# Layer 0's keys: turned once, copied to both partition halves by transfers, with the instruction order fitted anew

## Chip, core and metric

The kernel runs on one core of one Trainium2 chip. The metric is the time of one execution in device microseconds, start-up and end included. TensorE is called PE below, VectorE DVE, ScalarE ACT, GpSimd POOL and SyncE, which here only issues transfers, SP.

## What is computed

Two transformer layers over 512 tokens and a width of 1024, in float32. Layer 0 projects the normed input at once to sparse attention (A), with an indexer that picks 128 keys for each query, and to a sliding window attention (B). The keys are few: one head of A (`ak`), one of the indexer (`ik`), two of B (`bk`), 64 wide each, normed per head and rotated.

```python
ak = _rope(_rms_norm(ak.reshape(bsz, seq, 1, HEAD_DIM), a_k_gain), pos)[:, :, 0]
ik = _rope(_rms_norm(ik.reshape(bsz, seq, 1, IDX_DIM), idx_k_gain), pos)[:, :, 0]
bk = _rope(_rms_norm(bk.reshape(bsz, seq, B_KV_HEADS, HEAD_DIM), b_k_gain), pos)
...
rel = jax.nn.relu(jnp.einsum('bqhd,bsd->bqhs', qib, k_idx, preferred_element_type=jnp.float32))
score = jnp.einsum('bqhs,bqh->bqs', rel, wib.astype(jnp.float32)) * idx_scale
_, sel = lax.top_k(score, top_k)
```

Layer 1 has a dilated attention (C) and a differential attention (D) in the same places. After each layer a gated embedding is added to x.

## The kernel before

Every projection is split into a high and a low part of each operand and done as three products (`PASSES`), so that a weight slab of 128 rows (`raw`, 256 KB) is loaded by SP, split by ACT (high) and DVE (low) into `w`, and used by 12 matmuls of 512 columns: four output banks (`mm`, a ring of four) by three products.

`small_evac` takes the projection of the keys, one token tile of 128 after another in the order 1, 2, 3, 0. For each tile ACT copies 256 columns out of the bank, DVE and POOL norm them, DVE rotates them (`rope`) and writes the four heads **twice side by side** into a tile `z` of 512 columns, PE turns the four blocks of 128 columns (`tk`), and `put_heads` splits the bank of 512 columns, by ACT and by DVE, straight into `kTe`, the pair of tiles (high and low; `slot_145` and `slot_146` in the rows) that holds each key head in both halves of the partitions. The two halves are needed because the queries lie stacked, high in one half and low in the other. `scores` multiplies a query tile (`slot_113`, `slot_114` for the indexer) by the high and by the low keys into the banks `sk`, two of them in a ring.

The order of the instructions is not that of the text. `Program.add` records every call; `order` plays them through its own table of costs and lets each engine take the ready call of lowest rank. The rank is the place in the text minus a lead, which `LEADS` gives for each part of the program, 340 numbers in all. What each engine then executes is fixed, and so is SP's queue: a transfer that waits holds all behind it.

Between the projections of layer 0 stand the index scores (`index`), the selection on DVE (`select`, top 8 at a time) and the attentions (`attend_b`, `attend_a`). In layer 1 the queries of C (`put_far`) go to memory outside the core (`far`) and are fetched back, head pair by head pair, into tiles `q` (`fetch`).

The lines that the steps of the prediction touch:

```python
def put_heads(dst, t, bank):
    hi, lo = [d[:, :, t * P:(t + 1) * P] for d in dst]
    hilo(hi, lo, bank.rearrange("p (k n) -> p k n", k=4))
...
for c in range(2):
    nc.tensor.matmul(bank[:, :n], qT[j][:, p, qb * P:(qb + 1) * P],
                     kT[c][:, kv, key0 * P:key0 * P + n], start=c == 0, stop=c == 1)
```

Of the kernel before, what the change touches and what calls it, by code (L numbers as in the profile page):

```python
# [12 lines left out]
F32 = mybir.dt.float32  # L13
F32R = mybir.dt.float32r
BF16 = mybir.dt.bfloat16
AF = mybir.ActivationFunctionType
ALU = mybir.AluOpType
# [4 lines left out]
P = 128  # L22
# [4 lines left out]
HD = 64  # L27
# [1 line left out]
BIG = 1.0e30  # L29
GONE = -3.0e38  # L30
LEADS = {
    "att": (4, -1, -195, 26, -126, -326, 0, 214, 0, -171, 2, -255, 491, 23, 86, 12, -149, -103, -372, -13, 0, 4, 0, 0,
# [6 lines left out]
    "idx": (33, 43, -69),  # L39
    "mm": (1, 0, 41, -21, 0, -176, 0, 52, -54, 153, 2, 35, 58, 30, 82, 132, 16, -89, 217, 26, 163, -16, 219, -103, 0,  # L40
         2, 0, 32, 0, 10),
    "norm": (-7, -21, -1139, -422, 0, 163, 0, -1317, 0, -65, -255, 143, -554, 273, -6, 8, -797, 9, 343, 0, 45, 356,
         -448, -537),
    "rows": (18, -35, -52, -88),
    "rs": (-21, 0, -68),
    "ss": (0, 163, 0, -7, -4, 5, -8, -12, -47, -11, -20, 23, -71, 120, -103, 27, 0, 119, 63, 0, 144, 4, -6, 7, -774,
         -11, 355, 173, 169, -114, 0, -21),
    "tab": (444, 0, -16, -8, -33, -399),
    "top": (0, -62, -529, -1020, 86, -1, -9, -2, 184, -26, -53, -1657),
    "w": (-65, 84, 19, 457, -62, -25, -203, -28, 45, -204, -236, -132, -266, -243, -190, -125, 17, 0, -9, 0, 23, 3, 0,  # L50
         0, 44, 0, -8, -1, 0, 0),
    "x": (0, 254),
    "y": (424, -60, -418, 188, -612, 0, 22, 1, 283, 500, 1278, -7, 3, -30, -328, -184),
    None: -21,
}
VECS = ("a_q_gain", "a_k_gain", "idx_k_gain", "b_q_gain", "b_k_gain", "c_q_gain", "c_k_gain", "d_q_gain", "d_k_gain",
        "d_lambda_q1", "d_lambda_k1", "d_lambda_q2", "d_lambda_k2")
# [4 lines left out]
QB = 2  # L62
# [200 lines left out]
def tile_trunk(ctx: ExitStack, tc: tile.TileContext, a: dict, out: bass.AP):  # L263
    nc = Program(tc)

    const = ctx.enter_context(tc.tile_pool(name="const", bufs=1))
    sb = ctx.enter_context(tc.tile_pool(name="sb", bufs=2))
# [5 lines left out]
    def uid(s):  # L273
        cnt[0] += 1
        return f"{s}{cnt[0]}"
# [4 lines left out]
    def t_bank():  # L280
        return ps.tile([P, 512], F32, name=uid("tk"), tag="tk", bufs=1)
# [10 lines left out]
    def tmp(shape=(P, 512), tag="t", bufs=4, dt=F32):  # L292
        return sb.tile(list(shape), dt, name=uid(tag), tag=tag, bufs=bufs)
# [22 lines left out]
    ident = const.tile([P, P], F32, name="ident")  # L316
# [19 lines left out]
    def hilo(hi, lo, src, gain=None):  # L336
        if gain is None:
            nc.scalar.copy(out=hi, in_=src)
            nc.vector.tensor_tensor(out=lo, in0=src, in1=hi.bitcast(F32), op=ALU.subtract)
        else:  # L340
            nc.scalar.activation(out=hi, in_=src, func=AF.Copy, scale=gain)
            nc.vector.scalar_tensor_tensor(out=lo, in0=src, scalar=gain, in1=hi.bitcast(F32),
                                           op0=ALU.mult, op1=ALU.subtract)
# [206 lines left out]
    def rope(raw, nh, tabc, tabs, normed):  # L550
        if normed:
            sq = tmp()
            nc.scalar.activation(out=sq[:, :nh * HD], in_=raw, func=AF.Square)
            ss = tiny(nh)
            nc.vector.tensor_reduce(out=ss, in_=sq[:, :nh * HD].rearrange("p (h d) -> p h d", h=nh),
                                    axis=AX.X, op=ALU.add)
            hs = rs_pow(ss, nh, HD * EPS)
        else:
            hs = None
        t1 = tmp()  # L560
        t2 = tmp()
        nc.vector.tensor_tensor(out=t1[:, :nh * HD].rearrange("p (h d) -> p h d", h=nh),
                                in0=raw.rearrange("p (h d) -> p h d", h=nh), in1=tabc, op=ALU.mult)
        nc.vector.tensor_tensor(out=t2[:, :nh * HD].rearrange("p (h s d) -> p h s d", h=nh, s=2),
                                in0=raw.rearrange("p (h s d) -> p h s d", h=nh, s=2)[:, :, ::-1, :],
                                in1=tabs.rearrange("p h (s d) -> p h s d", s=2), op=ALU.mult)
        nc.vector.tensor_tensor(out=t1[:, :nh * HD], in0=t1[:, :nh * HD], in1=t2[:, :nh * HD], op=ALU.add)
        return t1, hs

    def heads():  # L570
        return [slot([P, 4, T], F32R) for _ in range(2)]
# [260 lines left out]
    for i in range(2):  # L832
        wr = slot([P, 4, 512])
        nc.sync.dma_start(out=wr[:, :, :456],
                          in_=a["w_small"][i * 512:(i + 1) * 512, :].rearrange("(k p) n -> p k n", p=P))
# [19 lines left out]
    kTe = heads()  # L855
# [5 lines left out]
    def small_evac(t, bank):  # L861
        raw = tmp(tag="raww", bufs=2)
        nc.scalar.activation(out=raw[:, :256], in_=bank[:, :256], func=AF.Copy, scale=rs0[:, t:t + 1])
        nc.scalar.activation(out=Ve[:, (1 + 3 * t) * HD:(4 + 3 * t) * HD], in_=bank[:, 256:448], func=AF.Copy,
                             scale=rs0[:, t:t + 1])
        nc.scalar.activation(out=iw[:, t, :], in_=bank[:, 448:456], func=AF.Copy, scale=rs0[:, t:t + 1])
        y, hs = rope(raw[:, :256], 4, ktab[:, 0, t], ktab[:, 1, t], True)
        z = tmp()
        nc.vector.tensor_tensor(out=z.rearrange("p (h u d) -> p h u d", h=4, u=2),
                                in0=y[:, :256].rearrange("p (h d) -> p h d", h=4).unsqueeze(2).to_broadcast([P, 4, 2, HD]),  # L870
                                in1=hs.unsqueeze(2).unsqueeze(3).to_broadcast([P, 4, 2, HD]), op=ALU.mult)
        b = t_bank()
        for i in range(4):
            nc.tensor.transpose(b[:, i * P:(i + 1) * P], z[:, i * P:(i + 1) * P], ident)
        put_heads(kTe, t, b)

    proj_tok(wsmall, small_evac, order="tok", tiles=(1, 2, 3, 0))

    few = sb.tile([P, 5 * P], F32, name="few", tag="acc12", bufs=1)
# [55 lines left out]
    idx = {qb: index(qb) for qb in (1, 2, 3)}  # L935
# [230 lines left out]
```

## Time and profile before

| | |
|---|---|
| median of 3 runs | 665.43 us (664.82 to 665.44) |
| the profiled execution | 664.71 us, of which its span is 662.8 us |
| PE busy | 654.7 us, 3373 matmuls |
| DVE, ACT, POOL busy | 530.0, 415.1, 63.4 us |
| granted clock of PE | 1.00 all through |

The span runs from the first to the last instruction. Matmuls overlap, so that a PE busy all the time may still stand between two of them; where it stood is read from the starts.

### The profile page before, as it was taken

What the parts mean: (1) busy time and instruction counts of PE and PEld (TensorE: products, weight loads), DVE (VectorE), ACT (ScalarE), POOL (GpSimd) and SP (SyncE); (2) the same over time, 40 slices, a digit from 0 to 9 for tenths busy, and PEclk for the clock granted to TensorE, in tenths of its full rate; (3) what the DMA queues carried; (4) which work ended last, traced back from release to release, by engine and by line L of the source; (5) the groups of instructions that cost most, each with busy time, mean ns of one, the idle gap of its engine ahead of it and who ended that gap; (6) DMA issues with size and microseconds to landing.
All of it is one profiled execution on the core that took longest, in us unless ns stands there. A gap on an engine that the chain in (4) does not pass through costs nothing.

```text
span 662.8 us, 10361 instructions
## 1 busy us (share of the span) xinstructions
PE 654.7 (99%) x3373; PEld 543.9 (82%) x3373; DVE 530.0 (80%) x1246; ACT 415.1 (63%) x937; POOL 63.4 (10%) x46
## 2 busy tenths in 40 slices
PE   9999999999999999999999999999999999999997
PEld 5888787988988888888888877888888888888886
DVE  6799999999997657677678395999997699558555
ACT  6757577989997824565455252885756577466421
POOL 0130232010000000000031040003040000000000
PEclk9999999999999999999999999999999999999999
DMA  9945256352533422342526537454757533341411
GB/s 332 336 101 145 81 136 182 119 137 65 176 95 97 143 84 77 112 146 93 160 78 182 151 113 223 118 153 113 235 158 206 164 115 94 112 117 58 128 64 64
DMA packets 76711, 90.49 MB, mean 137 GB/s; under 512 B 6641, under 2 KB 43889, under 8 KB 76401
## 3 DMA queue, kind: packets, MB, share of 16 engines
q1 hardware_dynamic: 76512, 89.81, 45.0%
q8 instruction: 27, 0.44, 0.3%
q14 instruction: 28, 0.22, 0.1%
q10 hardware_dynamic: 144, 0.02, 0.0%
HBM read 69.36 MB, written 10.49 MB: 120 GB/s over the span
## 4 chain that ended last, share of the span: by engine, by line
PE 88%; DVE 5%; DMA 3%; issue 1%; ACT 1%; POOL 0%; SPq 0%; DVEq 0%
PE mm L259 68%; PE ob L259 7%; PE tk L259 7%; PE sk L259 6%; DMA raw<-in_w_in_even_dram 1%; DVE t L259 1%; DMA q<-far 1%; DVE w L259 1%; DVE acc L259 1%; DVE few L259 1%; DMA raw<-in_w_ple_proj_dram 1%; POOL tiny L259 0%; SPq L259 0%; DMA far<-ql 0%; ACT w L259 0%
## 5 line engine op out<-in xcount | busy, mean ns | idle before, releaser
L259 PE MATMUL mm<-AT,w 128*128 128x512 f32 (+1 forms) x1176 | 291.0, 393 | 0.0
L259 PEld LDWEIGHTS mm<-AT,w 128*128 128x128 f32 x1176 | 212.6, 188 | 40.4 <-ACT t L259 0.2
L259 PE MATMUL mm<-w,AT 128*128 128x512 f32 (+1 forms) x936 | 238.7, 398 | 0.5 <-DVE w L259 0.5
L259 PEld LDWEIGHTS mm<-w,AT 128*128 128x128 f32 x936 | 170.4, 188 | 35.4 <-ACT AT L259 0.7
L259 ACT ACTIVATE w<-raw,gains 128x512 fp32r<-128x512 f32 x96 | 67.8, 720 | 59.4 <-PE mm L259 50.3
L259 DVE SCALAR_TENSOR_TENSOR w<-raw,gains,w 128x512 fp32r<-128x512 f32 x96 | 70.6, 747 | 28.9 <-ACT w L259 28.5
L259 POOL TENSOR_TENSOR tiny<-tiny,mhalf 128x8 f32<-128x8 f32 (+1 forms) x32 | 57.0, 1784 | 317.2 <-DVE tiny L259 291.9
L259 ACT ACTIVATE pr<-pr,nm 128x256 f32<-128x256 f32 (+3 forms) x128 | 68.5, 537 | 14.5 <-DVE nm L259 14.2
L259 ACT CAST w<-raw 128x512 fp32r<-128x512 f32 x79 | 48.0, 619 | 31.5 <-PE mm L259 21.9
L259 DVE TENSOR_TENSOR w<-raw,w 128x512 fp32r<-128x512 f32 x80 | 53.9, 686 | 13.9 <-ACT w L259 13.8
L259 PE MATMUL tk<-ident,pr 128*128 128x128 f32 x256 | 43.1, 273 | 0.0
L259 PE MATMUL sk<-slot,slot 128*128 128x256 f32 (+3 forms) x176 | 41.3, 323 | 0.0
L259 ACT ACTIVATE t<-t 128x512 f32<-128x512 f32 (+1 forms) x33 | 20.2, 615 | 31.0 <-DVE t L259 31.0
L259 PEld LDWEIGHTS ob<-pt,Ve 128*128 128x128 f32 x272 | 36.3, 191 | 3.5 <-ACT pt L259 1.3
L259 PE MATMUL ob<-pt,Ve 128*128 128x128 f32 x272 | 38.5, 276 | 0.4 <-ACT pt L259 0.4
L259 DVE CUSTOM_DVE_ANT_0 pr<-sk,cpack 128x128 f32<-128x128 f32 (+3 forms) x72 | 31.6, 463 | 8.7 <-PE sk L259 8.5
L259 DVE TENSOR_TENSOR t<-raww,tab 128x512 f32<-128x512 f32 x48 | 32.2, 684 | 6.4 <-ACT raww L259 6.1
L259 PEld LDWEIGHTS tk<-ident,pr 128*128 128x128 f32 x256 | 31.5, 141 | 6.1 <-ACT pt L259 0.9
L259 DVE TENSOR_TENSOR t<-mm,rows 128x512 f32<-128x512 f32 (+1 forms) x33 | 22.1, 670 | 14.5 <-PE mm L259 9.7
L259 PEld LDWEIGHTS sk<-slot,slot 128*128 128x128 f32 x176 | 28.7, 189 | 4.9 <-ACT t L259 1.0
L259 ACT COPY pt<-tk 128x512 f32<-128x512 f32 (+3 forms) x56 | 27.3, 488 | 8.5 <-PE tk L259 8.2
L259 DVE TENSOR_TENSOR AT<-slot,AT 128x512 fp32r<-128x512 f32 x40 | 26.9, 686 | 5.3 <-PE mm L259 3.1
(112 smaller groups left out, 806.9 us busy)
## 6 DMA issues: line engine op xcount, KB each, us to landing
raw<-in_w_in_odd_dram SPq DMA_DIRECT2D x64, 256.0 KB, 3.0
raw<-in_w_in_even_dram SPq DMA_DIRECT2D x36, 256.0 KB, 3.2
raw<-in_w_ple_gate_dram SPq DMA_DIRECT2D x32, 256.0 KB, 2.6
q<-far SPq DMA_DIRECT2D x64, 128.0 KB, 3.0
slot<-qh SPq DMA_DIRECT2D x38, 128.0 KB, 2.5
slot<-ql SPq DMA_DIRECT2D x38, 128.0 KB, 2.5
raw<-in_w_out_even_dram SPq DMA_DIRECT2D x16, 256.0 KB, 2.7
raw<-in_w_out_odd_dram SPq DMA_DIRECT2D x16, 256.0 KB, 2.6
```

The costliest lines, as they stand in the source:

```text
L259: getattr(getattr(nc, engine), method)(*args, **kw)
```

## The change

The heads are no longer doubled before the turn. `small_evac` writes the 256 columns once, PE turns two blocks, ACT and DVE split 256 columns into two tiles of the rings `qh` and `ql` (two buffers each, which the queries use too), and eight transfers of 64 partitions bring the two parts, head by head, into both halves of `kTe`. All 340 leads are other numbers, so the whole order moves; of them the first rows are shown.

```diff
 LEADS = {
-    "att": (4, -1, -195, 26, -126, -326, 0, 214, 0, -171, 2, -255, 491, 23, 86, 12, -149, -103, -372, -13, 0, 4, 0, 0,
+    "att": (-356, 8, 0, -362, 3, 213, 0, 36, 2, 14, -4, 0, 111, 0, 0, 166, 44, 3, -398, 0, 0, 10, 8, -1, -2, 0, 115,
...
         y, hs = rope(raw[:, :256], 4, ktab[:, 0, t], ktab[:, 1, t], True)
-        z = tmp()
-        nc.vector.tensor_tensor(out=z.rearrange("p (h u d) -> p h u d", h=4, u=2),
-                                in0=y[:, :256].rearrange("p (h d) -> p h d", h=4).unsqueeze(2).to_broadcast([P, 4, 2, HD]),
-                                in1=hs.unsqueeze(2).unsqueeze(3).to_broadcast([P, 4, 2, HD]), op=ALU.mult)
+        y = y[:, :256]
+        nc.vector.tensor_tensor(out=y.rearrange("p (h d) -> p h d", h=4), in0=y.rearrange("p (h d) -> p h d", h=4),
+                                in1=hs.unsqueeze(2).to_broadcast([P, 4, HD]), op=ALU.mult)
         b = t_bank()
-        for i in range(4):
-            nc.tensor.transpose(b[:, i * P:(i + 1) * P], z[:, i * P:(i + 1) * P], ident)
-        put_heads(kTe, t, b)
+        for i in range(2):
+            nc.tensor.transpose(b[:, i * P:(i + 1) * P], y[:, i * P:(i + 1) * P], ident)
+        parts = [sb.tile([P, 4, P], F32R, name=uid(x), tag=x, bufs=QB) for x in ("qh", "ql")]
+        hilo(parts[0][:, :2], parts[1][:, :2], b[:, :256].rearrange("p (k n) -> p k n", k=2))
+        for d, part in zip(kTe, parts):
+            for u in range(2):
+                for j in range(2):
+                    nc.sync.dma_start(out=d[64 * u:64 * u + 64, j::2, t * P:(t + 1) * P].bitcast(F32),
+                                      in_=part[64 * j:64 * j + 64, :2, :].bitcast(F32))
```

PE before, from the turn of the last key tile (`tk_187`) to the first index scores; `mm_279` to `mm_282` are the banks of the query projection of B:

```order
L259 MATMUL tk_187<-ident,t_186 128x128 x4
L259 MATMUL mm_281<-w_200,AT 128x512 x2
L259 MATMUL mm_282<-w_200,AT 128x512 x3
L259 MATMUL mm_279<-w_202,AT 128x512
L259 MATMUL sk_213<-slot_145,slot_113 128x256
L259 MATMUL sk_214<-slot_145,slot_114 128x256
L259 MATMUL mm_279<-w_202,AT 128x512 x2
L259 MATMUL mm_280<-w_202,AT 128x512
L259 MATMUL sk_213<-slot_146,slot_113 128x256
```

PE now, the same place (`tk_189` turns the keys of tile 0, `tk_167` of tile 2, `tk_178` of tile 3):

```order
L260 MATMUL tk_189<-ident,t_187 128x128 x2
L260 MATMUL mm_286<-w_204,AT 128x512 x3
L260 MATMUL mm_283<-w_206,AT 128x512 x3
L260 MATMUL mm_284<-w_206,AT 128x512 x3
L260 MATMUL tk_167<-ident,t_165 128x128 x2
L260 MATMUL mm_285<-w_206,AT 128x512 x3
L260 MATMUL mm_286<-w_206,AT 128x512 x3
L260 MATMUL mm_283<-w_208,AT 128x512 x3
L260 MATMUL mm_284<-w_208,AT 128x512 x2
L260 MATMUL sk_217<-slot_145,slot_113 128x256
L260 MATMUL sk_218<-slot_145,slot_114 128x256
L260 MATMUL mm_284<-w_208,AT 128x512
```

Before, 6 matmuls stand between the turn and the first scores; now 20 and another turn. The low keys (`slot_146`) are first read 4 matmuls and the turn `tk_178` after that.

SP's queue now, where the keys' transfers stand (in the kernel before, the rows of the key tiles are not there, and the slabs `raw` follow one another):

```order
L260 DMA slot_145<-qh_157 64x2x128 x4
L260 DMA slot_146<-ql_158 64x2x128 x4
L260 DMA raw_211<-in_w_in_even_dram 128x512
L260 DMA raw_213<-in_w_in_even_dram 128x512
L260 DMA raw_215<-in_w_in_even_dram 128x512
L260 DMA raw_327<-in_w_in_even_dram 128x512
L260 DMA slot_145<-qh_190 64x2x128 x4
L260 DMA slot_146<-ql_191 64x2x128 x4
L260 DMA slot_145<-qh_168 64x2x128 x4
L260 DMA slot_146<-ql_169 64x2x128 x4
L260 DMA slot_145<-qh_179 64x2x128 x4
L260 DMA slot_146<-ql_180 64x2x128 x4
```

The 32 transfers stand in two blocks, one of 8 and one of 24, with four slabs between them.

SP's queue in layer 1 before, around the last token tile of C's queries (`far_1033` is tile 0, `far_1066` tile 3; `raw` slabs are of a later projection):

```order
L259 DMA far_1066<-ql_1065 128x512
L259 DMA far_1033<-qh_1031 128x512
L259 DMA raw_1291<-in_w_in_odd_dram 128x512
L259 DMA q_1099<-far_1066 64x4x128 x2
L259 DMA far_1033<-ql_1032 128x512
L259 DMA raw_1293<-in_w_in_odd_dram 128x512
L259 DMA q_1089<-far_1033 64x4x128 x2
```

And now (`far_1037` is tile 0, `far_1070` tile 3):

```order
L260 DMA far_1037<-qh_1035 128x512
L260 DMA far_1070<-ql_1069 128x512
L260 DMA raw_1297<-in_w_in_odd_dram 128x512
L260 DMA far_1037<-ql_1036 128x512
L260 DMA q_1103<-far_1070 64x4x128 x2
L260 DMA q_1093<-far_1037 64x4x128 x2
```

The low part of tile 0 stood behind a slab and the fetch of tile 3; now it stands behind a slab alone, and the fetch of tile 3 comes after it.

On PE, 48 matmuls of 512 columns stood between the turn of tile 0 and the scores that need it (`q_1089`); it is 42 and four of 256 now (`q_1093`). For tile 1, whose scores come first, it was 38, and is 49 now.

## Rows read from the trace of the kernel before

**Rows 1.** The profile's page: busy time, share of the span, instructions of each engine.

```profile
PE 654.7 (99%) x3373; PEld 543.9 (82%) x3373; DVE 530.0 (80%) x1246; ACT 415.1 (63%) x937; POOL 63.4 (10%) x46
```

**Rows 2.** Stretches: length, busy PE, PEld, DVE, ACT, POOL (instructions), clock, DMA share, GB/s.

```profile
60.00:80.00 20.00, 20.00 (x89) 16.06 (x88) 20.00 (x50) 13.49 (x25) 1.44 (x1) 1.00 0.19 54
160.00:180.00 20.00, 19.56 (x135) 17.67 (x134) 19.53 (x65) 19.14 (x60) 0.00 (x0) 1.00 0.63 184
234.00:400.00 166.00, 165.73 (x748) 134.59 (x747) 115.86 (x195) 79.91 (x129) 18.02 (x10) 1.00 0.41 122
```

**Rows 3.** Groups by form, PE: count | busy us, mean ns | idle before.

```profile
L259 PE MATMUL tk<-ident,t 128*128 128x128 f32 x140 | 22.9, 273 | 0.0
```

**Rows 4.** Timeline of PE, key projection: start, length, instruction, count.

```profile
37.51 3.35 PE L259 MATMUL mm<-w,AT 128*128 128x456 f32 x15
40.70 0.60 PE L259 MATMUL tk<-ident,t 128*128 128x128 f32 x4
41.05 2.51 PE L259 MATMUL mm<-w,AT 128*128 128x456 f32 x11
43.40 0.60 PE L259 MATMUL tk<-ident,t 128*128 128x128 f32 x4
43.76 1.99 PE L259 MATMUL mm<-w,AT 128*128 128x456 f32 x8
```

**Rows 5.** Timeline of PE at four places where it stood; in brackets idle time.

```profile
104.21 1.53 PE L259 MATMUL mm<-w,w 128*128 128x512 f32 x6
106.12 1.20 PE L259 MATMUL mm<-w,w 128*128 128x512 f32 x4 [0.37 <-ACT raww L259]
...
164.74 0.28 PE L259 MATMUL sk<-slot,slot 128*128 128x256 f32 x1
165.47 0.71 PE L259 MATMUL ob<-pt,Ve 128*128 128x128 f32 x4 [0.44 <-ACT pt L259]
...
397.28 1.64 PE L259 MATMUL mm<-AT,w 128*128 128x512 f32 x6
399.19 0.71 PE L259 MATMUL sk<-slot,q 128*128 128x256 f32 x4 [0.27 <-issue]
...
411.74 2.03 PE L259 MATMUL mm<-w,AT 128*128 128x512 f32 x8
414.07 0.63 PE L259 MATMUL sk<-slot,q 128*128 128x128 f32 x4 [0.30 <-DMA q<-far]
```

**Rows 6.** The chain that ended last, 100 to 106 us: start, length, what.

```profile
100.34 3.98 DMA raw<-in_w_ple_proj_dram
...
105.40 0.67 ACT raww L259
```

**Rows 7.** The same chain, 402 to 414 us.

```profile
402.21 0.44 PE tk L259 x4
...
407.69 2.80 DMA far<-ql
...
411.19 2.74 DMA q<-far
```

**Rows 8.** Groups by form, DVE, 20 to 62 us.

```profile
L259 DVE TENSOR_TENSOR t<-raww,slot 128x256 f32<-128x256 f32 x8 | 3.2, 418 | 0.0
L259 DVE TENSOR_TENSOR slot<-tk,slot 128x512 fp32r<-128x512 f32 x4 | 2.8, 688 | 0.0
```

**Rows 9.** Tiles qh and raw, 20 to 60 us: ns min/median/max, first and last start.

```profile
L259 SPq DMA_DIRECT2D slot<-qh x6: 590/604/702, 29.7 to 39.0; - x6
L259 ACT CAST qh<-tk x3: 587/587/593, 29.1 to 37.8; 128x512 fp32r<-128x512 f32 x3
...
DMA to landing us min/median/max: 2.4/2.4/2.5
...
L259 SPq DMA_DIRECT2D raw<-in_w_in_even_dram x15: 327/328/787, 22.0 to 59.3; - x15
```

**Rows 10.** Timeline of PE up to the first index scores.

```profile
47.31 2.81 PE L259 MATMUL mm<-w,AT 128*128 128x512 f32 x11
49.95 0.60 PE L259 MATMUL tk<-ident,t 128*128 128x128 f32 x4
50.31 1.65 PE L259 MATMUL mm<-w,AT 128*128 128x512 f32 x6
51.80 0.40 PE L259 MATMUL sk<-slot,slot 128*128 128x256 f32 x2
```

More of the change, by code (lines that the diff above doesn't have):

```diff
@@ L31 @@
 LEADS = {
-    "att": (4, -1, -195, 26, -126, -326, 0, 214, 0, -171, 2, -255, 491, 23, 86, 12, -149, -103, -372, -13, 0, 4, 0, 0,
[6 rows of a table removed]
[L39 to L54, printed above, removed]
+    "att": (-356, 8, 0, -362, 3, 213, 0, 36, 2, 14, -4, 0, 111, 0, 0, 166, 44, 3, -398, 0, 0, 10, 8, -1, -2, 0, 115,
[7 rows of a table added]
+    "idx": (0, -19, -140),
+    "mm": (744, -44, -5, -100, 0, -370, 0, -81, 79, -11, 156, 0, 63, 118, 85, 144, -94, 133, 380, 29, 160, -6, 224,
+         -111, 9, -8, -15, -6, -21, -7),
+    "norm": (99, 644, 67, 0, 1120, 0, -27, -2462, 0, 268, 118, 5, -132, 0, 653, 0, -273, 89, 0, -98, 66, 18, -83,
+         -661),
+    "rows": (-291, -6, -205, -110),
+    "rs": (48, -45, 0),
+    "ss": (56, 44, 20, 128, -125, 746, 0, 9, 0, 88, 0, 160, 2, 370, -83, 163, 257, 0, -6, -43, -94, 9, -21, 0, 0, 265,
+         207, 384, 166, 189, 43, 115),
+    "tab": (-75, 52, 267, 0, 0, 0),
+    "top": (1052, 338, -786, -922, 0, 0, 4, 9, 177, -8, -5, -306),
+    "w": (97, 232, 550, 471, 185, -84, -58, 22, -107, -1, -101, -3, -117, 0, 0, 0, 8, -19, 2, -56, -234, -3, -102, 0,
+         -43, 84, -50, -117, -68, -254),
+    "x": (-619, -91),
+    "y": (108, 650, 0, 321, 2, 0, 12, -131, 2, 57, 0, -74, 756, -1, -273, 1434),
+    None: 170,
 }
```

13 rows, old and new, of the table LEADS are left out of this document.

## The prediction

> **What bounds the kernel now.** I read the page first, then the stretches, then the starts of PE's matmuls. PE is busy 99% of the span [rows 1], and in the long stretches of projection nearly all of it [rows 2]. A matmul lasts longer than the step to the next one, so busy time hides short stands; the starts show them. Rows 10 give the step: eleven matmuls and six matmuls of 512 columns, each after four turns, take 2.64 and 1.49 us up to the next start, so five matmuls are 1.15 us, 0.23 us each. At that step PE has little to lose. I looked for larger gaps between starts and found four that a change of order can touch [rows 5]: 6 matmuls from 104.21 to 106.12 take 1.91 us where 1.38 would do, 0.53 lost; one of 256 columns from 164.74 to 165.47 takes 0.73 instead of 0.12, 0.61 lost; 6 matmuls before 399.19 and 8 before 414.07 lose 0.5 each. That is 2.1 us together. So the time is the sum of PE's steps and about 2 us of stands, with a start and an end that the change leaves as they are. DVE is the second engine: it is busy 20.00 of 20 us from 60 to 80 and 19.53 from 160 to 180 [rows 2], where it selects keys, and ACT joins it there (19.14). Work taken from DVE or ACT pays only where PE waits for it.
>
> **The turns.** Eight of the sixteen go. Rows 4 give the price: from 37.51 to 41.05 there are 15 matmuls and 4 turns in 3.54 us, from 41.05 to 43.76 there are 11 and 4 in 2.71, so a matmul of 456 columns is 0.21 us, and four turns are 0.43 us, 0.108 each. Eight are 0.86 us, and as PE goes from one to the next without a pause, all of it is on the path. A turn's own length is 273 ns [rows 3], but it overlaps the next. The Trainium skill, "TensorE: Matmul & The Clock Gate", Part 4 (PE-mode transpose), gives about 275 ns for a transpose in a kernel; the length agrees, and eight would be 2.2 us by it. The step decides, and the sum goes by 0.86.
>
> **DVE and ACT.** For each of four tiles the multiply that wrote 512 columns and the subtraction of 512 write 256 now: 688 ns becomes 418 [rows 8], 0.27 us each, 2.2 us for the eight. ACT's cast of 512 columns is 587 ns [rows 9] and gets shorter as well. I cost this at nothing: PE's matmuls hide it, except where DVE's selection ends late. It gives slack up to 200 us, and no time by itself.
>
> **The transfers.** They put a new chain between the turn and the index scores: ACT's cast, SP's issues, landing. Before, the cast wrote the keys in place, and 1.85 us after the turn at 49.95 the first scores ran [rows 10]. What hides the chain now is the order: 20 matmuls and two pairs of turns, 20 x 0.23 + 0.43 = 5.0 us, up to the high keys, and 1.4 us more (four matmuls, a pair of turns, two score matmuls of 256) up to the low keys. The chain: the cast starts about 0.5 us after the turn (the last one, at 37.8, began 0.3 after the end of its four turns at 37.51 [rows 4, 9], and two turns are 0.2), lasts 0.3 to 0.59, and then eight issues follow one another on SP, and the last lands 2.4 us after its issue [rows 9]. The trace has no transfer of 64 partitions by two runs. The nearest rows are the slab, of 128 runs like the new ones, 0.33 us of issue, and the queries' transfer of 64 partitions by four runs, 0.60 [rows 9]. With a gap of 0.05 that makes a step of 0.38 or 0.65. At 0.38 the fourth issue lands at 0.9 + 1.1 + 2.4 = 4.4 us (5.0 to spare it) and the eighth at 6.0 (of 6.4): no wait. At 0.65 they land at 5.3 and 7.9: PE waits 0.3, then 1.5 in all. Tile 2 comes eight issues later; its low keys would land 13.1 us after the turn where the order has them read at 10.5, so 2.6 in all; tile 3 has 17 us for 18.3 and so is covered by that wait. So the price is 0 to 2.6 us. I take 0, since the number of runs is the slab's. A gain of its own is excluded, as nothing waits for less. Behind the 24 issues on SP stand four slabs and more for the next projection, which has 8 others in hand; SP is held some 9 us at 0.38, and the slabs before them in the queue wait for DVE's splits, which come before `ql_191` on DVE. The rings `qh` and `ql` make DVE wait for landings at the fourth tile, where few microseconds of other splits stand before it.
>
> The Trainium skill, "DMA: Bandwidth & Descriptors", Rules for kernel authors, speaks against this form: two transfers to disjoint halves of the partitions serialize, and one over 128 partitions is better. No run here shows the two side by side; by that rule the eight would run one after another, and its outcome is the third case below.
>
> **The order.** Some 340 leads move everything from 30 us on. Where PE's four stands are, I followed the new order:
> - 105 us: PE waited for ACT to empty a bank at 105.40, behind a split whose slab came at 104.3 [rows 6]. Now the banks are emptied without a slab's split between them, 3.5 us after the last matmul of the bank asked for. About 0.5 gone, at worst 0.1 left.
> - 399 us: 11 more matmuls, 2.5 us, stand between the turn of tile 1 and its scores. The 0.5 is gone.
> - 414 us: the chain was turn at 402.21, low part to memory at 407.69 for 2.80, fetch at 411.19 for 2.74 [rows 7]; 5.5 us passed before SP came to the low part. Now SP holds it behind one slab that needs a DVE split after a bank that ends 7 matmuls after the turn: 0.43 + 1.6 + 0.2 + two DVE steps of 0.69 + 0.33 = 4.0; with 2.80, a first fetch of 0.60 and 2.74 that is 10.1 to 10.3 us. PE gets there after 0.43 + 42 x 0.23 + 4 x 0.12 = 10.6. The 0.5 is gone, with 0.3 to spare.
> - 165 us: PE waits for ACT, which is full there before and after. I leave it.
>
> That is 1.5 us. The order moves many other places that I couldn't follow to the tenth, so I put one new stand of the usual size, 0.6, against it. Sum: -0.86 - 1.5 + 0.6 = -1.8 us, and 664.71 of the profiled execution becomes 662.9. That execution is 0.72 below the median of the runs, so the forecast is 663.7 us, 0.26% faster. About 0.2% (1.3 us) is what a measurement of this kernel can tell from no change.
>
> **Rivals.**
> 1. *The turns alone.* The new order has as many stands as the old, in other places: every wait I cleared is of 0.5 us, and the rows show four that a fit left standing. Then -0.86 alone: 664.6, no measurable change. For it: the order from 80 to 230 us is quite another one. Against it: two of the four cleared places have over 1 us of new cover.
> 2. *DVE's and ACT's relief reaches PE.* All four stands go and none comes: -0.86 - 2.1 = -3.0, and with short stands gone too, 662.0 to 661.5. For it: DVE is full from 60 to 200 us and gets 2.2 us back. Against it: PE hardly waits for DVE.
> 3. *The keys come late* (slower). SP's step for a transfer of 64 partitions is 0.65, not 0.38, since what counts is not the runs but the form. PE waits 2.6 us at the index scores: -0.86 + 2.6 = +1.7, without the order's gain 667.2. It decides from a step of about 0.45 on: 6.4 - 2.4 - 0.9 us leave 3.1 for seven steps. For it: the nearest row of the same half-partition form is at 0.60. Against it: four slabs and others with 128 runs are at 0.33.
>
> **How the numbers follow.** Forecast 0.45, the turns alone 0.30, relief 0.10, late keys 0.15. Time 663.7. The range leaves out the lower half of the relief case and half of the late keys, and some of the spread of the rest: 661.9 to 667.0. Faster by over 0.2% (below 664.1) is three quarters of the forecast and the relief case, 0.45; within 0.2% is the rest of the forecast, most of the turns alone, and a part of the late keys, 0.40; slower (above 666.8) 0.15.
>
> **What would show it.** In the profile after: PE at one step of 0.23 from the turn of tile 0 to the scores, with no idle time that ends on a transfer of the keys; SP's issues of the new transfers 0.33 long and 0.38 apart, landing in 2.4; 132 turns of `t`; no gap before the fetched scores near 400 and 415 us. I am wrong if PE's idle time names those transfers, if the new attention order between 80 and 230 us shows several gaps over 0.4 us, or if the gaps at 399 and 414 us stand elsewhere.

## The result: 0.8% slower

The changed kernel takes 671.6 us (median of 6 runs, 670.96 to 671.72), the kernel before 665.88 in the same comparison: a ratio of 1.008, 95% interval 1.0066 to 1.0094. The profiled execution took 671.68 us, with a span of 669.8; before it was 664.71 and 662.8. The forecast was 663.7 with a range up to 667.0, so the time lies outside it and on the other side.

The page of the changed kernel: busy time, share of the span and instructions of each engine, to be read against [rows 1]. PE has its eight turns less and is busy 2.1 us longer.

```profile
PE 656.8 (98%) x3365; PEld 545.3 (81%) x3365; DVE 529.2 (79%) x1246; ACT 417.1 (62%) x937; POOL 62.8 (9%) x46
```

The groups that the change touches, PE and DVE of the changed kernel by form (count | busy us, mean ns | idle before): 132 turns and not 140 [rows 3], and the subtraction at 256 columns, 420 ns and not 688 [rows 8]; the multiply is at 422.

```profile
L260 PE MATMUL tk<-ident,t 128*128 128x128 f32 x132 | 21.5, 275 | 0.0
...
L260 DVE TENSOR_TENSOR ql<-tk,qh 128x256 fp32r<-128x256 f32 x4 | 1.7, 420 | 2.7 <-ACT qh L260 2.7
```

**Where the time went.** I took the start of each of PE's matmuls, subtracted the start before, and from that the step of its width as it is in the kernel before (0.2285 us for 512 columns, 0.2055 for 456, 0.175 for 384, 0.118 for 256, 0.1085 for 128; nine matmuls at the start of the program have 0.427 and 24 of one column 0.028). The steps add up to 640.37 us before and 639.50 after: 0.87 less, the eight turns. What goes beyond the steps, in us:

| stretch | 0-40 | 40-80 | 80-140 | 140-380 | 380-440 | 440-end | sum |
|---|---|---|---|---|---|---|---|
| before | 1.26 | 0.87 | 1.86 | 5.41 | 2.27 | 4.46 | 16.12 |
| the change | 1.14 | 7.21 | 1.16 | 5.41 | 3.18 | 5.88 | 23.95 |

So 6.3 us come between 40 and 80 us and 2.3 in layer 1; 0.9 goes with the turns and 0.7 at 80 to 140. Together 7.0, the whole difference of the two profiled executions.

PE of the changed kernel around the first index scores (timeline; the bracket is idle time and what ended it). Before, the scores followed the turn without a gap [rows 10]; now PE stands 3.08 us for the high keys, and four matmuls from 57.44 and three from 59.55 then take 1.26 and 1.28 us where 0.91 and 0.69 would do.

```profile
48.78 0.38 PE L260 MATMUL tk<-ident,t 128*128 128x128 f32 x2
...
51.24 2.81 PE L260 MATMUL mm<-w,AT 128*128 128x512 f32 x11
57.12 0.48 PE L260 MATMUL sk<-slot,slot 128*128 128x256 f32 x2 [3.08 <-DMA slot<-qh]
57.44 1.45 PE L260 MATMUL mm<-w,AT 128*128 128x512 f32 x4
58.70 0.63 PE L260 MATMUL tk<-ident,t 128*128 128x128 f32 x2
58.98 0.77 PE L260 MATMUL sk<-slot,slot 128*128 128x256 f32 x2
59.55 1.48 PE L260 MATMUL mm<-w,AT 128*128 128x512 f32 x3
...
71.46 0.39 PE L260 MATMUL mm<-w,AT 128*128 128x512 f32 x1
72.89 0.50 PE L260 MATMUL sk<-slot,slot 128*128 128x512 f32 x1 [1.04 <-ACT t L260]
```

SyncE's issues in the same stretch (SPq in the rows; timeline: start, time from the first issue of a row to the end of its last, transfers). Four key transfers take 2.54 us, so the step is 0.65; one issue, the last of the row at 51.22, lasts 1.23. From 43.85 to 68.03 the queue has no gap over 0.51 us. The turn of tile 0 is at 48.78, its cast ends at 49.57, and its first transfer is issued at 51.22, behind the low keys of tile 1 and four slabs.

```profile
43.85 2.54 SPq L260 DMA_DIRECT2D slot<-qh  x4
46.50 2.54 SPq L260 DMA_DIRECT2D slot<-ql  x4
49.08 2.04 SPq L260 DMA_DIRECT2D raw<-in_w_in_even_dram  x4
51.22 3.17 SPq L260 DMA_DIRECT2D slot<-qh  x4
54.90 2.54 SPq L260 DMA_DIRECT2D slot<-ql  x4
...
68.03 7.35 SPq L260 DMA_DIRECT2D raw<-in_w_in_even_dram  x7
```

Stretches of the changed kernel (columns as in [rows 2]; the clock is the third number from the end). In the first microsecond after the stand (57 to 58) the granted clock is 0.98; then it is 0.50, the lower of its two levels, and PE makes 11 matmuls in 3 us.

```profile
54.00:57.00 3.00, 0.04 (x1) 0.00 (x0) 1.76 (x6) 1.24 (x2) 0.00 (x0) 1.00 0.40 106
...
58.00:61.00 3.00, 3.00 (x11) 2.40 (x10) 1.12 (x3) 0.94 (x3) 0.00 (x0) 0.50 0.42 103
```

The chain of the changed kernel around the two waits. First: the fourth high transfer is issued at 53.16 and lands 3.72 us later, behind two of the slabs. Second: SyncE comes to the next slabs only at 68.03, ACT has to split one before it empties a score bank, and PE waits for that bank.

```profile
53.16 3.72 DMA slot<-qh
...
57.12 0.48 PE sk L260 x2
```

```profile
68.67 3.14 DMA raw<-in_w_in_even_dram
...
71.83 0.02 ACT w L260
...
72.35 0.49 ACT t L260
...
72.89 0.50 PE sk L260
```

The 16 high transfers of the changed kernel, by their buffer (ns min/median/max, first and last start; then us from issue to landing): most land after 2.0 us.

```profile
L260 SPq DMA_DIRECT2D slot<-qh x16: 590/604/1228, 43.9 to 64.7; - x16
...
DMA to landing us min/median/max: 2.0/2.1/5.0
```

So the 6.3 us are 3.24 and 1.20 for the two waits (by the steps), 0.24 for the low keys at 58.98, 1.4 for the lower clock (what the other matmuls from 57.12 to 61.55 take beyond their steps), and 0.2 in small pieces.

### The profile page after: what moved, and what is told of

Same layout as the page of the kernel before. It is cut to its first block, busy times and chain, and to the rows that moved or that the text cites. A ratio compares the mean times of both kernels' runs of the same rounds, so it can differ in the third digit from the quotient of the medians.

```text
span 669.8 us, 10393 instructions
## 1 busy us (share of the span) xinstructions
PE 656.8 (98%) x3365; PEld 545.3 (81%) x3365; DVE 529.2 (79%) x1246; ACT 417.1 (62%) x937; POOL 62.8 (9%) x46
## 4 chain that ended last, share of the span: by engine, by line
PE 84%; DVE 7%; DMA 4%; issue 2%; SPq 1%; ACT 1%; DVEq 0%
PE mm L260 65%; PE ob L260 8%; PE tk L260 6%; PE sk L260 5%; DVE t L260 2%; DMA q<-far 2%; DVE pr L260 1%; DVE w L260 1%; SPq L260 1%; DVE tiny L260 1%; DVE slot L260 1%; DMA raw<-in_w_out_odd_dram 1%; DMA slot<-qh 1%; DMA far<-ql 1%; DVE few L260 1%
## 5 line engine op out<-in xcount | busy, mean ns | idle before, releaser
L260 PE MATMUL mm<-w,AT 128*128 128x512 f32 (+1 forms) x936 | 241.9, 399 | 0.0
L260 PEld LDWEIGHTS mm<-w,AT 128*128 128x128 f32 x936 | 172.5, 190 | 34.0 <-ACT AT L260 0.6
L260 PEld LDWEIGHTS ob<-pt,Ve 128*128 128x128 f32 x272 | 34.5, 191 | 3.5 <-ACT pt L260 2.0
L260 PE MATMUL ob<-pt,Ve 128*128 128x128 f32 x272 | 37.1, 277 | 0.0
L260 ACT CAST qh<-tk 128x512 fp32r<-128x512 f32 (+1 forms) x31 | 17.3, 558 | 24.7 <-PE tk L260 18.0
```

The costliest lines, as they stand in the source:

```text
L260: getattr(getattr(nc, engine), method)(*args, **kw)
```

## The experiments

**Keys or order?** Two kernels swap the tables of leads, each is one part of the change alone.

```diff
 newkeys_oldorder: the change's small_evac
-LEADS of the change
+LEADS of the kernel before
 oldkeys_neworder: the kernel before
-LEADS of the kernel before
+LEADS of the change
```

> The change's code for the keys (two turns and 32 transfers), with the table of leads of the kernel before. Theory S (SyncE): the loss between 40 and 80 us is made by the transfers themselves, 0.65 us of issue each on a queue that also carries the weight slabs; then PE waits here too for over 2 us in that stretch on transfers from qh or ql or on what comes behind them, its clock falls once behind it, and the time is 667 to 672. Theory O (order): the new leads make the loss; then these keys cost nothing with the old leads and the time is 664.0 to 665.5, the eight turns being 0.87 us.

> The kernel before with the change's table of leads: sixteen turns, keys written in place, no new transfer. Theory S: nothing holds PE at the first scores, no fall of its clock after 20 us, and what is left of the loss is that of layer 1 (some 0.8 us more near 410 us and 0.8 near 551 us than before): 665.5 to 667.5. Theory O: the waits of 3.2 us near 54 and 1.2 us near 71 us stay, with the fall of the clock: 670 to 673.

Measured: the new keys with the old leads 685.34 us, ratio 1.0297 (1.0281 to 1.0312); the old keys with the new leads 666.79, ratio 1.0021 (1.0013 to 1.0030). The direction is that of the transfers (S), the size of the first was missed by 13 us. The old leads give the transfers little cover, and PE stands twice for them:

```profile
62.70 0.77 PE L259 MATMUL sk<-slot,slot 128*128 128x256 f32 x2 [5.53 <-DMA slot<-qh]
65.36 0.77 PE L259 MATMUL sk<-slot,slot 128*128 128x256 f32 x2 [1.89 <-DMA slot<-ql]
```

In the first, 12.2 us are lost over the steps at 40 to 80 us and 9.9 at 80 to 140, where the change loses 7.2 and 1.2. So with the new leads the same keys are some 14 us faster than with the old: 5.0 us of it lie where the keys are awaited, 8.7 behind, where every order that was planned anew with these keys loses (below); how much of that the transfers themselves make isn't shown. In the second, 40 to 80 us is as before (0.97 us over the steps) and layer 1 loses 1.7 more. The new leads by themselves cost 1.2.

**Fewer transfers.** ACT and DVE write the half that already lies on the right partitions; 16 transfers remain, 4 a tile and not 8.

```diff
-        parts = [sb.tile(...) for x in ("qh", "ql")]
-        hilo(parts[0][:, :2], parts[1][:, :2], b[:, :256]...)
-        ...
+        for u in (1, 0):
+            own, other = [slice(64 * i, 64 * i + 64) for i in (u, 1 - u)]
+            hilo(kTe[0][own, u::2, at], kTe[1][own, u::2, at], b[own, :256]...)
+            for d in kTe:
+                nc.sync.dma_start(out=d[other, u::2, at]..., in_=d[own, u::2, at]...)
```

> The change with its leads, but ACT and DVE write each head's own half of the partitions in place, in two pieces of 64 partitions, and a transfer brings only the other half: 16 transfers and not 32, two of 64x2x128 before the index keys of a tile are there and not four, no ring of buffers behind them. Theory S: SyncE is held 10 us and not 21, the wait near 54 us falls below 0.5 us and that near 71 us goes, the clock stays whole: 665 to 667.5, layer 1's loss of some 1.6 us staying. Theory O: 670 to 672, as the leads are the change's.

> Own halves in place and 16 transfers, with the leads of the kernel before. Theory S: PE waits less than half as long for keys as with 32 transfers and these leads; if it waits for none the time is 664.0 to 665.5 (eight turns of 0.108 us less than before, and layer 1 as before). Theory O: the same 664.0 to 665.5, and no difference from 32 transfers with these leads.

Measured: 668.56, ratio 1.0056 (1.0035 to 1.0076), and 672.75, ratio 1.0112 (1.0099 to 1.0125). Half of the transfers, and the loss of 40 to 80 us falls from 7.2 to 2.7 (12.2 to 3.6 with the old leads). But both are slower than expected: with the change's leads 1.2 us of wait remain at the first scores, where less than 0.5 was expected, and 3.0 us are lost at 80 to 140, where the change loses 1.2 (with the old leads 6.3, and 9.9 with 32 transfers).

**What an issue costs.** 28 further transfers from one spare buffer to others, four of each of seven forms, at the end of the kernel before's text. The planner put them between 593 and 647 us, some of them between weight slabs, so they do not all stand back to back.

```diff
+    nc.sync.dma_start(out=d1[:, i, :], in_=s[:, i, :])                                      # 128x512
+    nc.sync.dma_start(out=d2[64*u:64*u+64, j::2, :P], in_=s[64*j:64*j+64, :2, :P])          # 64x2x128
+    (128x2x128, 64x128, 64x512, 128x128, 64x4x128 likewise)
```

> The kernel before with 28 more transfers behind its end, from one spare buffer into four others, back to back on SyncE, four of each form: 128x512 in one run, 64x2x128 (the change's), 128x2x128, 64x128, 64x512, 128x128, 64x4x128; the time is of no interest, the length of each issue is. If the number of runs counts, as the prediction had it: 0.33 us for 64x2x128, 64x128, 64x512, 128x128 and 128x512, 0.6 for 128x2x128 and 64x4x128. If half of the partitions counts: 0.6 for the four forms of 64, 0.33 to 0.43 for those of 128. If several runs in a partition count: 0.6 for 64x2x128, 128x2x128 and 64x4x128, 0.33 to 0.43 for the one-run forms.

Measured: none of the three; 23 of the 28 last 0.58 to 0.64 us, some of every form. All the transfers and, for comparison, those that go to the output (ns, min/median/max):

```profile
L259 SPq DMA_DIRECT2D slot<-slot x28: 462/604/1838, 592.9 to 646.3; - x28
L259 SPq DMA_DIRECT2D out_dram<-slot x9: 332/332/343, 631.6 to 660.3; - x9
```

Eight that stand together, four of 64x512 and four of 128x128, take 4.96 us, and four of 64x4x128 take 2.67: 0.62 and 0.67 each.

```profile
607.64 4.96 SPq L259 DMA_DIRECT2D slot<-slot  x8
...
644.26 2.67 SPq L259 DMA_DIRECT2D slot<-slot  x4
```

So neither the runs nor the partitions nor the bytes (32 to 256 KB) set the issue. A transfer from buffer to buffer costs SyncE some 0.6 us; the slab at 0.33 [rows 9] comes from memory. The fetches of layer 1, from memory as well, are at 0.6, so memory alone does not decide. And 0.33 is the slab that stands alone. In the kernel before, at 1.2 to 4.0 us, where issues from memory follow one another, a slab lasts 0.43 and the step is 0.48 (tile raw, SyncE, 0 to 5 us: ns min/median/max, first and last start):

```profile
L259 SPq DMA_DIRECT2D raw<-in_w_in_even_dram x4: 421/432/435, 1.2 to 4.0; - x4
```

The first slab behind transfers from buffer to buffer lasts 0.59 in the changed kernel (at 49.08 and 68.03). So what stands just ahead in the queue counts too; what decides is open.

**Another queue.** Half of the transfers issued by ACT or by POOL, with the order planned anew; and the planner told the right price.

```diff
 half_on_act_queue, half_on_pool_queue
-                    nc.sync.dma_start(out=d[64 * u:64 * u + 64, j::2, ...
+                    (nc.scalar if u else nc.sync).dma_start(...      # or nc.gpsimd
 planner_price_650
-            return 450
+            return 650 if reads and reads[0].space != DRAM and writes and writes[0].ap[0][1] == 64 else 450
```

> The change, but the 16 transfers to the upper half of the partitions are issued by ACT and 16 by SyncE; ACT waits in line for DVE's low parts. If SyncE's 0.65 us per transfer makes the loss of 40 to 80 us: SyncE is held 10 us, the wait near 54 us falls by 1 to 3 us, that near 71 us shrinks, 667 to 670, unless ACT, 0.6 us per issue, now holds the index scores. If SyncE is not the cause: 671 to 672.

> The change, but the 16 transfers to the upper half of the partitions are issued by POOL, which is nearly idle there, and 16 by SyncE. If SyncE's 0.65 us per transfer makes the loss of 40 to 80 us: the wait near 54 us falls by 1 to 3 us and that near 71 us goes, 666.5 to 669.5; a longer issue or landing on POOL's queue would give part of it back. If SyncE is not the cause: 671 to 672.

> The change with the same leads, but the planner prices a transfer of 64 partitions between buffers at 650 ns of SyncE and not 450; only the order follows. If the order was planned with too short an issue, more matmuls of the projection now stand ahead of the first scores: the wait near 54 us falls by 1 us or more, 668 to 670.5; the queue stays as long, so that near 71 us stays. If the planner's price does not matter: 671 to 672.

Measured: 671.68 (ratio 1.0102, 1.0079 to 1.0124), 669.2 (1.0058, 1.0035 to 1.0081) and 675.12 (1.0139, 1.0116 to 1.0162). POOL's time lies in the range for SyncE's issues as the cause, ACT's in the one against it, the planner's above both. But over the steps PE loses 4.6, 1.5 and 3.2 us at 40 to 80 us, all less than 7.2. ACT issues in line with its casts: from the cast of the keys, which ends at 50.65, to the next cast at 53.62 it does nothing but issue, which the bracket shows as idle time:

```profile
52.32 1.26 ACTq L260 DMA_DIRECT2D slot<-ql  x2
53.62 0.62 ACT L260 CAST w<-raw 128x512 fp32r<-128x512 f32 x1 [2.96 <-DMA slot<-qh]
```

And each of the three loses at 80 to 140 us most of what it gained, or more: 3.8, 5.6 and 7.1 us there, where the change loses 1.2. The right price cut the wait at the first scores to 0.75 us, as expected, and still did not help. The leads had been fitted with the wrong price; that this is the reason was not tested.

**Four more variants.** layer1_oldorder takes the leads of the kernel before from layer 1's first projection on; index_heads_first sends the index key's half of each tile first; the last two issue all 16 transfers of own_half_direct on POOL, the second also with the old leads for layer 1.

```diff
 layer1_oldorder, own_half_pool_layer1_old
+    nc.leads, nc.lead = LEADS_1, LEADS_1[None]
     ckT = heads()
 index_heads_first
+        for j in (1, 0):
             for d, part in zip(kTe, parts):
 own_half_pool_queue, own_half_pool_layer1_old: on own_half_direct
-                nc.sync.dma_start(out=d[other, u::2, at]...
+                nc.gpsimd.dma_start(out=d[other, u::2, at]...
```

> The change with its own leads for layer 0 and the leads of the kernel before from layer 1's first projection on. If the waits near 410, 429, 517 and 551 us (1.66, 0.43, 0.50 and 0.82 us) come from the new leads of layer 1, they give way to those of the kernel before (0.44, 0.47, 0.35): 1.5 to 2.2 us less than the change, 669.4 to 670.2, with the loss between 40 and 80 us as it was. If they come from layer 0's delay or from the transfers: 671 to 672.

> The change with its 32 transfers in another order: of each tile the four that carry the index key's half first. If the queue on SyncE makes the first wait, the scores need the second transfer and not the fourth of the high keys: the wait near 54 us falls by 0.3 to 1.3 us, that near 59 us goes, the late slabs and the wait near 71 us stay: 669.5 to 671.3. If not: 671.3 to 672.

> Own halves written in place as before in own_half_direct, and the 16 transfers issued by POOL: SyncE issues no key at all. If the issue on SyncE was the whole loss of 40 to 80 us, less than 0.8 us is left there. What follows is open: with half of the transfers on POOL the loss of 40 to 80 us went but 4 us came at 120 to 140. If that is DVE and ACT, full from 80 us on, it comes here as well: 667 to 669.5; if it was the half on SyncE: 664.5 to 666.5.

> The kernel of own_half_pool_queue with the leads of the kernel before from layer 1's first projection on: 1.5 to 2.2 us less than it, 665 to 667.5, if layer 1's waits come from its leads; no difference if they come from elsewhere. Faster than the kernel before only if no wait is left at 120 to 140 us.

Measured: 672.59 (ratio 1.0091, 1.0076 to 1.0107), 674.03 (1.0120, 1.0102 to 1.0138), 669.46 (1.0051, 1.0033 to 1.0069), 670.01 (1.0053, 1.0035 to 1.0071). The first two lie above both of their ranges, the third is in its range, and the fourth shows no difference from the third. Layer 1 with its old leads loses 10.1 us over the steps from 380 us on, against 9.1 of the change and 6.7 of the kernel before: the old leads do not bring the old layer 1 back behind another layer 0. With the index keys first the wait at the scores stays, 3.09 us: they need the second transfer, issued at 51.66, and it lands at 56.0 behind the same slabs. Without any key on SyncE 1.6 us of wait remain (2.9 lost at 40 to 80, where less than 0.8 was expected): ACT casts tile 0's keys 1.2 us after the turn (48.87 and 50.03), behind the cast of a slab.

**The queue alone.** All variants so far had also a newly planned order. These two keep every engine's order. In half_pool_same_order the transfers are planned as SyncE's and 16 are handed to POOL; in slabs_behind_keys four issues move on SyncE.

```diff
 half_pool_same_order
+                    if u:
+                        nc.route.add(len(nc.calls) - 1)
...
-                    getattr(getattr(nc, engine), method)(*args, **kw)
+                    getattr(getattr(nc, "gpsimd" if i in self.route else engine), method)(*args, **kw)
 slabs_behind_keys (SyncE's order)
+DMA slot_145<-qh_190 64x2x128 x4
+DMA slot_146<-ql_191 64x2x128 x4
 DMA raw<-in_w_in_even_dram 128x512 x4
-DMA slot_145<-qh_190 64x2x128 x4
-DMA slot_146<-ql_191 64x2x128 x4
```

> The change with every engine's order left exactly as it is; only 16 of the 32 key transfers (those to the upper half) are issued by POOL, at the same place among the others. In half_on_pool_queue the planner had also made a new order, and 4 us came at 120 to 140 us. If SyncE's queue makes the loss of 40 to 80 us (7.2 us of PE's starts over the step, 0.9 in the kernel before), it falls below 2.5 here. If the 4 us at 120 to 140 came from the new order and not from full DVE and ACT, they stay away here: 665.5 to 667.5. If DVE and ACT are the next bound whatever the order, they come again: 668.5 to 670.

> The change with one edit of SyncE's order and none on the other engines: the four weight slabs between the keys of tile 1 and those of tile 0 stand behind the eight transfers of tile 0; their weights are used 10 us later or more. If the four slabs ahead of the keys (2 us of issue, and transfers in front of the keys' in the DMA engines) make a part of the wait near 54 us, it falls from 3.2 to 0 to 1.2 us, what is left being 0.65 a transfer. ACT's cast of tile 2's high keys stands behind two casts of those slabs, so that tile 2 and 3 come some 2 us later and the wait near 71 us grows by up to as much: 670 to 672.5 in all. If only the issue step counts and not the slabs: the wait near 54 us stays over 2.5 us.

Measured: 665.15 us (ratio 1.0007, 0.9988 to 1.0025) and 674.86 (1.0143, 1.0123 to 1.0162). The first is the decisive run. 16 issues moved, nothing else: 40 to 80 us is at 0.86 us over the steps, as in the kernel before, and 80 to 140 at 1.10. SyncE comes to tile 0's high keys at 49.70 and not at 51.22, and POOL issues two in 1.2 us beside it. With half of tile 1's keys gone from SyncE the four slabs leave it earlier too, from 46.62 and not from 49.08, and tile 0's high keys land after 2.6 to 3.1 us and not 3.7 to 5.0.

```profile
49.70 1.25 SPq L261 DMA_DIRECT2D slot<-qh  x2
...
49.97 1.22 POOL L261 DMA_DIRECT2D slot<-qh  x2 [0.94 <-ACT qh L261]
```

The stretches of half_pool_same_order: PE makes 18 matmuls and not 11 in the 3 us, at the full clock; and from 120 to 140 us it never stands.

```profile
58.00:61.00 3.00, 3.00 (x18) 2.48 (x18) 2.50 (x6) 2.32 (x6) 0.55 (x1) 1.00 0.87 210
...
120.00:140.00 20.00, 20.00 (x124) 17.59 (x124) 20.00 (x70) 19.90 (x62) 2.02 (x1) 1.00 0.54 143
```

The same stretch of half_on_pool_queue, where the same transfers were moved and the order planned anew: 106 matmuls. DVE and ACT are as full in the one as in the other, so it was the order.

```profile
120.00:140.00 20.00, 18.16 (x106) 15.60 (x106) 19.73 (x72) 19.77 (x60) 0.00 (x0) 0.91 0.42 121
```

slabs_behind_keys shows that the first wait needs the slabs ahead of the keys: all 32 transfers are on SyncE at the step of 0.65, tile 0's high keys are issued from 49.57 and land after 2.0 us each, and the scores start at 53.86 without any wait. The time is still 2.4 us above what was expected: ACT's cast of tile 2's keys stands behind casts of these slabs, and PE stands 8.3 us at tile 3's turn, where up to 2 us more were expected. Which places the four slabs could have had without this wasn't tried.

```profile
53.86 0.40 PE L276 MATMUL sk<-slot,slot 128*128 128x256 f32 x2
...
63.48 0.66 PE L276 MATMUL tk<-ident,t 128*128 128x128 f32 x2 [8.30 <-DVE t L276]
```

**Layer 1.** In the change the wait at 399 us [rows 5] stands at 410 and is larger. PE, then SyncE, of the changed kernel:

```profile
398.40 0.60 PE L260 MATMUL tk<-ident,t 128*128 128x128 f32 x4
...
407.93 2.55 PE L260 MATMUL mm<-AT,w 128*128 128x512 f32 x10
411.98 0.71 PE L260 MATMUL sk<-slot,q 128*128 128x256 f32 x4 [1.49 <-issue]
```

```profile
402.49 0.33 SPq L260 DMA_DIRECT2D raw<-in_w_in_odd_dram  x1
402.86 0.43 SPq L260 DMA_DIRECT2D far<-ql  x1
403.97 1.26 SPq L260 DMA_DIRECT2D q<-far  x2
405.33 0.55 SPq L260 DMA_DIRECT2D raw<-in_w_in_odd_dram  x1
405.98 0.38 SPq L260 DMA_DIRECT2D far<-qh  x1
406.44 1.29 SPq L260 DMA_DIRECT2D q<-far  x2
```

The low part of tile 1, subtracted by 400.6, is issued at 402.86, behind a slab that waits for DVE's split until 402.46; its fetches come at 406.44, behind those of tile 2, a slab and a store. Three kernels move these issues on SyncE and nothing else; half_pool_fetches_first does it for tile 0 as well.

```diff
 half_pool_fetch_first (on half_pool_same_order), change_fetch_first (on the change)
+DMA far_1048<-ql_1047 128x512
 DMA raw_1179<-in_w_in_odd_dram 128x512
-DMA far_1048<-ql_1047 128x512
 DMA q_1098<-far_1059 64x4x128 x2
+DMA q_1092<-far_1048 64x4x128 x2
 DMA raw_1293<-in_w_in_odd_dram 128x512
 DMA far_1070<-qh_1068 128x512
-DMA q_1092<-far_1048 64x4x128 x2
 half_pool_fetches_first, besides
+DMA far_1037<-ql_1036 128x512
 DMA raw_1297<-in_w_in_odd_dram 128x512
-DMA far_1037<-ql_1036 128x512
+DMA q_1093<-far_1037 64x4x128 x2
 DMA q_1103<-far_1070 64x4x128 x2
-DMA q_1093<-far_1037 64x4x128 x2
```

> The kernel of half_pool_same_order with one edit more on SyncE and none on the other engines: in layer 1 the low part of tile 1's queries goes to memory ahead of the weight slab that stands before it, and the two fetches of tile 1 stand right behind those of tile 2, ahead of one slab and one store. If the wait of 1.8 us near 404 us is that slab's split, behind which SyncE held the low part, and the place of the fetches: low part landing at 398.5 to 399 and not 399.9, last fetch at 403 to 404 and not 405.8, the wait below 0.4, and 1.4 to 1.8 us less than half_pool_same_order: 663.2 to 664.0, faster than the kernel before by 0.2 to 0.3%. If the fetches land late because of the slabs in the DMA engines (4.3 to 4.7 us of landing): no change or 0.5 us, 664.6 to 665.2.

> The change, all 32 transfers on SyncE, with the same edit of SyncE's order in layer 1 alone. If the wait near 410 us (1.66 us) is the slab's split and the place of the fetches: below 0.4, and 1.2 to 1.7 us less than the change, 669.9 to 670.5, with the loss between 40 and 80 us untouched. If not: 671 to 672.

> The kernel of half_pool_fetch_first, in which the wait near 404 us went and one of 1.2 us for tile 0's fetch stood near 413; with the same edit for tile 0: its low part ahead of the slab that stands before it on SyncE, its two fetches ahead of tile 3's. If SyncE's order makes this wait too, it falls below 0.4 us: 0.7 to 1.2 us less than half_pool_fetch_first, 663.2 to 663.8, unless tile 3's scores, some 10 matmuls later, now wait for their fetch: then no change, 664.2 to 664.8.

Measured: 664.44 (ratio 0.9987, 0.9974 to 0.9999), 670.9 (1.0090, 1.0071 to 1.0110) and 663.58 (0.9965, 0.9950 to 0.9980). In the first two the wait for tile 1's fetch goes, and the next fetch, tile 0's, becomes late instead, 1.2 us, so that less than half of the 1.7 us comes back:

```profile
414.25 0.64 PE L287 MATMUL sk<-slot,q 128*128 128x128 f32 x4 [1.19 <-DMA q<-far]
```

With both moved PE goes through (half_pool_fetches_first):

```profile
401.53 2.54 PE L295 MATMUL mm<-AT,w 128*128 128x512 f32 x10
403.91 0.64 PE L295 MATMUL sk<-slot,q 128*128 128x256 f32 x4
...
407.16 4.83 PE L295 MATMUL mm<-w,AT 128*128 128x512 f32 x20
411.82 0.56 PE L295 MATMUL sk<-slot,q 128*128 128x128 f32 x4
```

It loses 0.88 us over the steps at 40 to 80 us and 1.39 at 380 to 440 (2.27 before). This version, the change with 16 key transfers on POOL and six issues of SyncE moved, beats both kernels: 0.35% faster than the kernel before, and its interval does not reach 1.

## Why the prediction was wrong, step by step

- **What bounds the kernel**: right. PE's steps and stands make up the time in every run here, and the difference of any two profiled executions is found in its starts.
- **The turns**: right. 0.87 us by the steps, 0.86 forecast.
- **DVE and ACT**: right. The instructions have the lengths that were put down for them, and no time comes of it. PE's stands in fact starve DVE, which is busy 14.00 of 20 us from 40 to 60 and was 19.63 before.
- **The transfers**: the step that failed. The two bounds of the issue step were 0.38 and 0.65, and I took the lower by the number of runs; all 32 are at the upper, one of them longer. The forms run shows that the runs say nothing, and the nearest row was the one of the same kind, buffer to buffer [rows 9]. The lower bound was no price for a row of issues in any case: 0.33 is a slab alone, and the step of slabs in a row was 0.48 in the kernel before, above the 0.45 from which the rival was to decide. The rival *the keys come late* named the mechanism and had the place right, but it too was mis-sized: 2.6 us, where 6.3 came. Three terms were missing from it. The chain began with a free queue at tile 0's turn, where tile 1's low keys and four slabs still stood ahead of it: 1.6 us later at the first issue (51.22 for 49.57). The landing was put at 2.4 us: it is 2.0 for most of them, but 3.7 to 5.0 for tile 0's high keys behind those slabs, which slabs_behind_keys takes away together with the wait. These two and the 0.3 us that the rival gave to the high keys make up the first wait: 0.3, 1.65 for the queue and 1.32 for the landing (3.72 for 2.4) are 3.27, and 3.24 was measured. And a stand of 3 us costs more than itself: the clock fell to half behind it, 1.4 us, and the slabs that SyncE had held back made a second wait at 71 us, 1.2 us. The slabs behind the keys were seen in the prediction and thought to be covered by eight others; ACT, which must split them ahead of emptying a score bank, was not thought of.
- The Trainium skill's rule against two transfers to disjoint halves ("DMA: Bandwidth & Descriptors", Rules for kernel authors) pointed the right way. But it speaks of engines that the transfers share, and here most land 2.0 us after their own issue, one 0.65 behind the other; it is the issues that stand in line. The next row of the same table of the Trainium skill fits better: it says that spreading transfers over SP, ACT and GpSimd brings no bandwidth and saves only issue time. Moving 16 issues was worth some 6 us here, from 671.6 to 665.15 (the kernel before at 665.88 and 665.29 in the two comparisons).
- **The order**: half right. (The table has 319 leads, not 340, and 11 of them are as before.) The stand at 105 us went as forecast (0.7 us less at 80 to 140), and from 80 to 230 us, where many new gaps would have spoken against the forecast, the changed kernel has none over 0.3 us. That at 399 came back as 1.66: I counted PE's cover, 2.5 us more, and took the chain as it was, but in the new order the low part is issued 4.5 us after the turn and not 2.0, and the last fetch lands after 4.8 and not 3.9. What holds it is SyncE's order, which the last three runs show. The stand at 414 was hidden by the one before it and appeared as soon as that was taken away.
- **One new stand of 0.6**: too few. Behind 440 us the change loses 1.4 more, the largest stand 0.82 near 551 us, for a slab. Why the stretch behind 440 us loses more in all variants (5.0 to 8.4 us, before 4.46) is not settled; the new leads alone make 1.2 of it (oldkeys_neworder).
- **Relief reaches PE**: not seen in any run.
- **That the order is fitted** was known, and how closely was not: each kernel whose layer 0 was planned anew with the new keys lost 1.8 to 8.8 us more than the change at 80 to 140 us, while those that kept the order lost nothing there.

With the two faults of SyncE's queue mended, the kernel is at 663.58 us, next to the forecast of 663.7. That is a coincidence and no support for the forecast, which had all 32 transfers on SyncE at no price and the order as it was planned; this kernel has three edits more.

## What to carry to other kernels

A queue that only issues is an engine like the others: sum up what it has to issue in the stretch, from the first instruction that can be ahead of the awaited one, at the price of the row of the same kind, with the same neighbours in the queue. Moving work off a full PE onto SyncE pays only if SyncE has room just there; if it hasn't, an idle engine's queue beside it, with the order left as it is, can take the loss away. And where a table of leads was fitted to a kernel, test an edit with the order held fixed, since a newly planned order changes more than the edit.

## What the runs showed of the hardware that I had not expected

- The length of an issue on SyncE did not follow runs, partitions or bytes: of seven forms from 64x128 to 128x512, buffer to buffer, 23 of 28 issues took 0.58 to 0.64 us (forms), stores to memory 0.33.
- It depends on what the queue issued just before: a slab of 256 KB took 0.33 us alone [rows 9], 0.43 in a row of issues from memory (the kernel before, 1.2 to 4.0 us), and 0.59 as the first behind transfers from buffer to buffer (the changed kernel, 49.08 and 68.03).
- A transfer's landing depends on what was issued ahead of it: 2.0 us with no slab just ahead, 3.7 to 5.0 behind four slabs of 256 KB (the changed kernel and slabs_behind_keys).
- After 3.1 us without a matmul PE's granted clock was 0.98 from 57 to 58 us and 0.50 from 58 to 61. It was alike behind the 3.09 us of index_heads_first (0.95 from 56 to 57, 0.50 from 57 to 60); behind the 1.63 us of own_half_pool_queue it stayed at 1.00.
- POOL issues such a transfer in 0.6 us as well, in parallel with SyncE: 16 on each, with the order held, took away the whole loss of 40 to 80 us.
